# A hybrid decoder block on one core: a fixed order for the output projection, weight loads divided between two queues, rotary steps on VectorE, and compression low parts by adding DMA

## The chip, the cores and the metric

One core of one Trainium2 chip. The metric is the device time of one execution in microseconds, the median of several runs. A second execution is recorded by the hardware profiler, and all rows shown come from it. Engines are named PE (TensorE matmul), PEld (TensorE weight load), DVE (VectorE), ACT (ScalarE), POOL (GpSimd) and SP (SyncE, which here only issues DMAs).

## The reference

512 tokens of width 2048 pass one decoder block. A conditioning vector gives shift, scale and gate vectors (`mod`); one projection feeds two groups of eight heads, forgetting attention (FoX) and native sparse attention (NSA), whose outputs are normalised, concatenated and projected.

```python
def _compress(x, cmp_pos, w1, w2, idx):          # NSA, once for keys, once for values
    blk = x[:, idx] + cmp_pos[None, None, :, None, :]
    blk = blk.transpose(0, 1, 3, 2, 4).reshape(B, idx.shape[0], G, CMP_LEN * D)
    return jax.nn.gelu(blk @ w1) @ w2
...
    mod = jax.nn.silu(c) @ w_ada[l] + b_ada[l]
    sh1, sc1, g1, sh2, sc2, g2 = jnp.split(mod, 6, axis=-1)
    u = _modulate(_rmsnorm(h, norm_attn[l]), sh1, sc1)
    z = u @ w_in                                   # 16 heads' queries, keys, values, gates
    y_f = _rmsnorm(o_f.reshape(B, S, FOX_HEADS * HEAD_DIM), beta_fox)
    y_n = _rmsnorm(o_n.reshape(B, S, NSA_HEADS * HEAD_DIM), beta_nsa)
    h = h + g1[:, None, :] * (concatenate([y_f, y_n]) @ w_out)
    u = _modulate(_rmsnorm(h, norm_ffn[l]), sh2, sc2)
    h = h + g2[:, None, :] * _swiglu(u, w_gate[l], w_up[l], w_down[l])
```

The NSA queries and two of its key sets are rotated (`_rope`). D_MODEL 2048, 8 + 8 heads of 128, compression weights of 32 x 128 rows by 256 columns for keys and again for values, D_FF 5632.

## The kernel before

Activations lie with channels on partitions and 512 tokens along the free axis. Every large product is made of three matmuls on operands split in two: a high part, rounded by an ACT copy (`wh`, `uh`, L244), and a low part, the rest, by a DVE subtraction (`wl`, L249). `gemm` (L289) walks over pieces `ct` of 256 input rows: `load_w` (through `fetch_w`, L218) loads a weight piece on SP's queue into one of three buffers `wr` and splits it, then the matmuls follow. Between pieces `pump` takes a step of a side job: `side_ada` makes the modulation vectors (`ada_block`, L380 loads 512 KB, L386 multiplies and adds on DVE), `side_cmp` the compressions, `att` the attention items, `side_mix` the normalised head outputs. Up to the output projection the scheduler orders each engine's instructions by the program and by when they can be ready; a queue runs its own in order.

The places that the change touches, in time order:

- `z_qn(0)` (L727), queries of the first four NSA heads. `roped` (L606) takes four heads one after another: two ACT copies of the swapped halves, a DVE product (L611), two POOL steps (L612, L613), an ACT high part (L615) and a DVE low part (L616).
- The value products `p_v0` (L744), eight pieces with 288 columns, with `compress` (keys, then values, L655) pumped beside them. A compression has 16 steps: each loads 256 KB (`w1`, L672, on SP), splits it (`evac_pair`, L621 on ACT and L622 on DVE) into a pair from a ring of six (`pair("k", 6, ...)`) and feeds six matmuls (L678). Three of the six pairs hold keys at that time.
- The last value GEMM (`pr == 3`). `mix_hook` pumps `mix_nsa`, which reloads an NSA head's output from DRAM (`reload`, L956, SP), multiplies it by the row scale on POOL (`mix_chunk`, L948) and makes `y`'s high part on ACT (L950) and low part on DVE (L951).
- The output projection. Groups of four or two column blocks of 128 (`out_group`). The first halves of g0 and g1 (rows 8 to 15 of y, the NSA heads) run before the attention pools close; g1's hook `fox_hook` reloads and mixes the FoX heads, every other one on POOL. Then the loop L1193 finishes g0 and g1 and does three whole groups; `x_hook` reloads the hidden state (`hT`, from `xsp`, on SP) and in the last two groups starts the feed-forward's first weights (`w_load`, `w_sums`, `x_high`, `x_low`, `s_split`). After each group `res_add` (L1064, DVE) adds the gated residual, and `hT` is stored to `hsd` by POOL.
- From there a fixed program order (`manual_schedule`) holds for the feed-forward. Its low parts `lx` are made by an ACT pass with factor -1 (L1096) and a POOL DMA that adds the raw weights (L1097).

Of the kernel before, what the change touches and what calls it, by code (L numbers as in the profile page):

```python
# [79 lines left out]
def hymba_block(ctx: ExitStack, tc: tile.TileContext, x, c, positions, w_ada, b_ada, norm_attn,  # L80
# [525 lines left out]
    def roped(src, dst, scale, ct, snt, n):  # L606
# [5 lines left out]
        nc.gpsimd.tensor_tensor(sw, sw, snt, op=OP.mult)  # L612
        nc.gpsimd.tensor_tensor(r, r, sw, op=OP.add)  # L613
# [40 lines left out]
    def compress(which, w1, w2d):  # L654
        hb = bank("s", (P, 256))  # L655
        for s in range(2):
# [26 lines left out]
        nc.sync.dma_start(w2, w2d.rearrange("(m p) n -> p m n", p=P))  # L683
# [43 lines left out]
    def z_qn(g, nxt, **kw):  # L727
        Z = [bank("mm") for _ in range(4)]
        gemm([cols(w_in, C_QN + 512 * g, 512)], u, ND, [("ws", i * P, P, Z[i]) for i in range(4)], **kw)
        w = nxt()  # L730
        if g == 0:
            for i in range(4):
                nc.vector.tensor_tensor(part[:, i, :], part[:, i, :], Z[i], op=OP.add)
        for i in range(4):
            qn[4 * g + i] = pair("q", 6, "qn")
            roped(part[:, i, :] if g == 0 else Z[i], qn[4 * g + i], SCALE, cosT, sinT, T)
        return w
# [5 lines left out]
    w_v0 = z_qn(0, lambda: ahead(p_v0, extra=wsm), k0=ND // 2, start=ND // 2, first=z_first)  # L743
# [5 lines left out]
    gemm(p_v0, u, ND, [("as", 0, 288, bks)], extra=wsm, n_cmp=7, first=w_v0)  # L749
# [40 lines left out]
    side_ada.extend(ada_block(pa, sec, j) for sec, j in todo_ada[:9])  # L790
# [163 lines left out]
    def reload(i):  # L954
        o = sc_tile("or")
        nc.sync.dma_start(o, osp[i])  # L956
        return o
# [12 lines left out]
    def mix_hook(ct):  # L970
        if ct >= 1:
            pump(side_mix, 1 if ct == 1 else 2)
# [38 lines left out]
    pump(side_mix, 1000)  # L1011

    def out_group(i0, n, tags):
        Z = [bank(t) for t in tags[:n]]
        return [cols(w_out, i0 * P, n * P)], y, ND, [("ws", m * P, P, Z[m]) for m in range(n)]

    order = list(range(8, 16)) + list(range(8))
    g0 = out_group(0, 4, BANKS_A)
    gemm(*g0, order=order, n_ada=1, n_att=1.25, k1=8)
    att.drain()  # L1020
    rb = rows_of(sum_rstd(osum[0], FH * HD, "o", "rsf"), "o", q_tmp("rbf"))
    fox = order[8:]

    def fox_hook(ct):
        for h in fox[2 * ct:2 * ct + 2]:
            mix_chunk(reload(h), h, rb)

    g1 = out_group(4, 2, BANKS_B)
    gemm(*g1, order=order, n_ada=1, k1=8, hook=fox_hook)
    pump(side_ada, 1000)  # L1030
# [45 lines left out]
    def w_load(s):  # L1076
        g, k = divmod(s, KG)
        c = slice(g * HT, (g + 1) * HT)
        raw[s] = ring1.tile([P, 4, HT], F32, tag="raw", name=uid("raw"), bufs=6)
        nc.sync.dma_start(raw[s][:, 0:2, :], wu_v[:, :, k, c])  # L1080
        nc.sync.dma_start(raw[s][:, 2:4, :], wg_v[:, :, k, c])
# [110 lines left out]
    side_ada.extend(ada_block(pf, sec, j) for sec, j in todo_ada[9:])  # L1192
    for i0, n, g in ((0, 4, g0), (4, 2, g1), (6, 4, BANKS_A), (10, 4, BANKS_B), (14, 2, BANKS_A)):  # L1193
        k0 = 8 if i0 < 6 else 0
        if i0 >= 6:
            g = out_group(i0, n, g)

        def x_hook(ct):
            if ct == k0 // 2 + 2:
                for i in range(i0, i0 + n):  # L1200
                    nc.sync.dma_start(hT[i], xsp[i])
            if i0 == 10 and 2 <= ct < 8:
                w_load(ct - 2)
            if i0 == 14:
                if ct == 2:
                    hsum["b"] = bank("s")
                    sum_tok(hsum, hsum["t"], True, False)
                if 1 <= ct < 3:
                    w_sums(ct - 1)
                if 1 <= ct < 4:  # L1210
                    x_high(ct - 1)
                if 1 <= ct < 5:
                    x_low(ct - 1)
                if 3 <= ct < 5:
                    s_split(ct - 3)
                if ct == 5:
                    w_sums(2)

        gemm(*g, order=order, k0=k0, hook=x_hook, n_ada=1)
        res_add(i0, [o[3] for o in g[3]], 2, hsum, "hsum")  # L1220
        for i in range(i0, i0 + n):
            nc.gpsimd.dma_start(hsd[i], hT[i])
# [8 lines left out]
    ms = ExitStack()  # L1231
    ms.enter_context(tc.manual_schedule())
# [194 lines left out]
```

## Time and profile before

| | us |
|---|---|
| runs of the kernel before | 2450.6, 2454.54, 2454.8 |
| their median | 2454.54 |
| the profiled execution | 2450.92 |
| its span in the trace | 2448.0 |
| TensorE busy in the span | 2355.1 (96%) |
| DVE, ACT, POOL busy | 1579.6, 1016.0, 341.5 |

The profiled execution's time is 2.9 us longer than its span, the part outside the first and last recorded instruction. A busy time is the sum of an engine's recorded instructions. The granted clock is given as a share of full speed: 1.00 is 2.4 GHz and a stretch at 0.50 would be all at 1.2 GHz. Stretches are named by microseconds from the span's start.

### The profile page before, as it was taken

What the parts mean: (1) busy time and instruction counts of PE and PEld (TensorE: products, weight loads), DVE (VectorE), ACT (ScalarE), POOL (GpSimd) and SP (SyncE); (2) the same over time, 40 slices, a digit from 0 to 9 for tenths busy, and PEclk for the clock granted to TensorE, in tenths of its full rate; (3) what the DMA queues carried; (4) which work ended last, traced back from release to release, by engine and by line L of the source; (5) the groups of instructions that cost most, each with busy time, mean ns of one, the idle gap of its engine ahead of it and who ended that gap; (6) DMA issues with size and microseconds to landing.
All of it is one profiled execution on the core that took longest, in us unless ns stands there. A gap on an engine that the chain in (4) does not pass through costs nothing.

```text
span 2448.0 us, 38482 instructions
## 1 busy us (share of the span) xinstructions
PE 2355.1 (96%) x14717; PEld 2100.4 (86%) x14717; DVE 1579.6 (65%) x2711; ACT 1016.0 (42%) x1531; POOL 341.5 (14%) x370
## 2 busy tenths in 40 slices
PE   6998999999999989889999999999999999999998
PEld 4677887888888767789999999999999888888887
DVE  6876786887755576596777777777776643333333
ACT  3224544344423332365555555555555422222133
POOL 0003002000001121251222121212221100000010
PEclk8998999999999999999999999999999999999999
DMA  9864743463554277559898989898988644333322
GB/s 332 283 198 147 205 139 95 130 190 117 180 174 129 85 249 253 186 122 237 211 231 215 228 213 232 220 225 212 221 200 193 192 151 141 123 120 121 102 95 101
DMA packets 322713, 440.31 MB, mean 180 GB/s; under 512 B 26224, under 2 KB 217552, under 8 KB 322528
## 3 DMA queue, kind: packets, MB, share of 16 engines
q1 hardware_dynamic: 289104, 348.21, 44.0%
q0 software_dynamic: 31120, 85.45, 18.7%
q10 hardware_dynamic: 2304, 4.20, 0.5%
q8 instruction: 115, 1.88, 0.3%
q14 instruction: 70, 0.57, 0.1%
HBM read 340.18 MB, written 28.38 MB: 151 GB/s over the span
## 4 chain that ended last, share of the span: by engine, by line
PE 54%; DVE 1%; DMA 0%; issue 0%; ACT 0%; SPq 0%; DVEq 0%; ACTq 0%
PE py L1161 12%; PE py L1164 11%; PE py L1163 11%; PE psmm L278 3%; PE psmm L279 3%; PE psmm L280 3%; PE pss L278 2%; PE pss L279 2%; PE pss L280 2%; PE pso L279 1%; PE pso L278 1%; PE pso L280 1%; DMA wr<-in_w_down_dram 0%; PE pso L1058 0%; DVE ul L1141 0%
## 5 line engine op out<-in xcount | busy, mean ns | idle before, releaser
L249 DVE TENSOR_TENSOR wl<-wr,wh 128x1024 fp32r<-128x1024 f32 (+2 forms) x211 | 239.0, 1133 | 381.5 <-ACT wh L244 378.4
L244 ACT CAST wh<-wr 128x1024 fp32r<-128x1024 f32 (+2 forms) x211 | 199.5, 948 | 502.7 <-PE psmm L279 199.7
L1164 PE MATMUL py<-uh,ls 128*128 128x256 f32 x1408 | 397.6, 282 | 3.6 <-DVE ls L1107 3.6
L1163 PE MATMUL py<-ul,hs 128*128 128x256 f32 x1408 | 397.6, 282 | 2.2 <-DVE ul L1141 2.2
L1161 PE MATMUL py<-uh,hs 128*128 128x256 f32 x1408 | 398.4, 283 | 1.0 <-DVE ev L1178 0.5
L1107 DVE TENSOR_TENSOR ls<-sum,hs 128x1024 fp32r<-128x1024 f32 x176 | 215.2, 1223 | 196.5 <-ACT hs L1101 196.5
L1101 ACT CAST hs<-sum 128x1024 fp32r<-128x1024 f32 x176 | 184.5, 1049 | 377.3 <-PE py L1163 257.5
L1163 PE MATMUL py<-ul,hx 128*128 128x256 f32 x1056 | 298.8, 283 | 4.0 <-DVE ul L1141 4.0
L1161 PE MATMUL py<-uh,hx 128*128 128x256 f32 x1056 | 299.3, 283 | 1.7 <-ACT uh L1140 1.4
L1164 PE MATMUL py<-uh,lx 128*128 128x256 f32 x1056 | 298.3, 282 | 0.0
L1164 PEld LDWEIGHTS py<-uh,ls 128*128 128x128 f32 x1408 | 267.0, 190 | 4.7 <-DVE ls L1107 4.6
L1163 PEld LDWEIGHTS py<-ul,hs 128*128 128x128 f32 x1408 | 267.0, 190 | 3.3 <-DVE ul L1141 3.3
L1161 PEld LDWEIGHTS py<-uh,hs 128*128 128x128 f32 x1408 | 267.1, 190 | 2.7 <-DVE ev L1178 1.3
L1097 POOL DMA_DIRECT2D lx<-raw x176 | 156.2, 887 | 580.2 <-ACT lx L1096 419.4
L1163 PEld LDWEIGHTS py<-ul,hx 128*128 128x128 f32 x1056 | 200.8, 190 | 5.1 <-DVE ul L1141 5.1
L1161 PEld LDWEIGHTS py<-uh,hx 128*128 128x128 f32 x1056 | 200.6, 190 | 2.2 <-ACT uh L1140 1.7
L1164 PEld LDWEIGHTS py<-uh,lx 128*128 128x128 f32 x1056 | 200.7, 190 | 0.0
L386 DVE SCALAR_TENSOR_TENSOR acc<-ad,sl,acc 128x512 f32<-128x512 f32 x180 | 141.6, 787 | 43.2 <-DMA ad<-in_w_ada_dram 41.4
L1092 ACT CAST hx<-raw 128x768 fp32r<-128x768 f32 x176 | 144.3, 820 | 11.3 <-DMA raw<-in_w_gate_dram 11.3
L1096 ACT ACTIVATE lx<-raw 128x768 fp32r<-128x768 f32 x176 | 148.1, 841 | 1.8 <-DMA raw<-in_w_gate_dram 1.8
L278 PE MATMUL psmm<-fh,wh 128*128 128x512 f32 x352 | 137.0, 389 | 0.0
L280 PE MATMUL psmm<-fh,wl 128*128 128x512 f32 x352 | 136.9, 389 | 0.0
(441 smaller groups left out, 5284.3 us busy)
## 6 DMA issues: line engine op xcount, KB each, us to landing
lx<-raw POOLq DMA_DIRECT2D x176, 384.0 KB, 5.2
ad<-in_w_ada_dram SPq DMA_DIRECT2D x128, 512.0 KB, 4.1
raw<-in_w_up_dram SPq DMA_DIRECT2D x176, 256.0 KB, 4.2
raw<-in_w_gate_dram SPq DMA_DIRECT2D x176, 256.0 KB, 4.5
wr<-in_w_down_dram SPq DMA_DIRECT2D x88, 512.0 KB, 3.6
ad<-in_w_ada_dram SPq DMA_DIRECT2D x128, 256.0 KB, 6.0
wr<-in_w_in_dram SPq DMA_DIRECT2D x104, 256.0 KB, 3.5
wr<-in_w_in_dram SPq DMA_DIRECT2D x24, 512.0 KB, 4.4
```

Source lines behind the costliest of these rows:

```text
L244: nc.scalar.copy(wh[:, :, sc], v)
L249: nc.vector.tensor_tensor(held[1][:, :, sc], v, split_ap(held[0])[:, :, sc], op=OP.subtract)
L278: nc.tensor.matmul(dst, wh[:, k, w], ah, start=first, stop=False)
L279: nc.tensor.matmul(dst, wh[:, k, w], al, start=False, stop=False)
L280: nc.tensor.matmul(dst, wl[:, k, w], ah, start=False, stop=last)
L1096: nc.scalar.activation(lx[s], raw[s][:, 1:4, :], AF.Copy, scale=-1.0)
L1097: nc.gpsimd.dma_start(split_ap(lx[s]), raw[s][:, 1:4, :], accum_op=OP.add)
L1101: nc.scalar.copy(hs[s], sums[s])
L1107: nc.vector.tensor_tensor(ls[s], sums[s], split_ap(hs[s]), op=OP.subtract)
L1161: nc.tensor.matmul(o, wh[:, wi, js], vh[:, vi, :], start=k == 0 and j == 0, stop=False, skip_group_check=True)
L1163: nc.tensor.matmul(o, wh[:, wi, js], vl[:, vi, :], start=False, stop=False, skip_group_check=True)
L1164: nc.tensor.matmul(o, wl[:, wi, js], vh[:, vi, :], start=False, stop=k == KG - 1, skip_group_check=True)
```

## The change

1. Ropes: for the first four NSA heads the two POOL steps go to DVE, and each head's rope is emitted behind one of the first four pieces of the value products. Two of these pieces are loaded ahead, not one.
2. Compression: its weights are loaded by POOL's queue. For every second step the low part is made by a second ACT pass (factor -1) and a POOL DMA that adds the raw weights; the other steps keep the DVE subtraction. Steps are pumped from the fifth piece of the value products on (nine a piece), not from the second and third (seven).
3. One chunk of NSA output per piece in the last value GEMM, not two; the rest in the first w_out group. Reloads go on POOL's queue. Ten modulation blocks before w_out, not nine.
4. From g1 on the fixed program order holds: weight pieces loaded and split one ahead, FoX heads in pairs on DVE alone, the residual of a group after the first products of the next, hidden-state reloads and the first six feed-forward weight pieces on POOL's queue.

```diff
-            pump(side_cmp, n_cmp if ct > 1 else ct)
+            pump(side_cmp, n_cmp if ct > 3 else 0)
...
-    def roped(src, dst, scale, ct, snt, n):
+    def roped(src, dst, scale, ct, snt, n, eng=None):
...
-        nc.gpsimd.tensor_tensor(sw, sw, snt, op=OP.mult)
-        nc.gpsimd.tensor_tensor(r, r, sw, op=OP.add)
+        eng.tensor_tensor(sw, sw, snt, op=OP.mult)
+        eng.tensor_tensor(r, r, sw, op=OP.add)
...
-                nc.sync.dma_start(wr.rearrange("p (l n) -> p l n", n=256),
+                nc.gpsimd.dma_start(wr.rearrange("p (l n) -> p l n", n=256),
...
-                evac_pair(wr, w)
+                if l0 % 4:
+                    nc.scalar.copy(w[0], wr)
+                    nc.scalar.activation(w[1], wr, AF.Copy, scale=-1.0)
+                    nc.gpsimd.dma_start(split_ap(w[1]), wr, accum_op=OP.add)
+                else:
+                    evac_pair(wr, w)
...
-    w_v0 = z_qn(0, lambda: ahead(p_v0, extra=wsm), ...)
+    w_v0, rope_hook = z_qn(0, lambda: ahead(p_v0, extra=wsm) + ahead(p_v0, 1, extra=wsm), ...)
-    gemm(p_v0, u, ND, [("as", 0, 288, bks)], extra=wsm, n_cmp=7, first=w_v0)
+    gemm(p_v0, u, ND, [("as", 0, 288, bks)], extra=wsm, n_cmp=9, first=w_v0, hook=rope_hook)
...
-    side_ada.extend(ada_block(pa, sec, j) for sec, j in todo_ada[:9])
+    side_ada.extend(ada_block(pa, sec, j) for sec, j in todo_ada[:10])
...
     def reload(i):
-        nc.sync.dma_start(o, osp[i])
+        nc.gpsimd.dma_start(o, osp[i])
...
-            pump(side_mix, 1 if ct == 1 else 2)
+            pump(side_mix, 1)
...
+    ms.enter_context(tc.manual_schedule())
+    fox = {h: reload(h) for h in range(4)}
+    g1 = out_group(*groups[1])
+    products(g1, 0, w1[0])
+    r = sum_rstd(osum[0], FH * HD, "o", "rsf")
+    w1.append(load_out(4, 2))
+    products(g1, 1, w1[1])
+    rb = rows_of(r, "o", q_tmp("rbf"))
...
+    w1.append(load_out(4, 3))
+    fox_pair(0)
+    products(g1, 2, w1[2])
+    w0 = [load_out(0, 4)]
+    fox_pair(2)
...
     def w_load(s):
+        eng = nc.gpsimd if s < 6 else nc.sync
...
+        for ct in range(c0, 8):
+            if ct < 7:
+                nw = load_out(i0, ct + 1)
+            elif n_grp < 4:
+                nw = load_out(groups[n_grp + 1][0], starts[n_grp + 1])
+            pump(side_ada, ct in n_ada.get(i0, ()))
+            products(g, ct, w)
+            w = nw
+            if ct == c0 and owed is not None:
+                owed()
+            if ct == (7 if i0 == 0 else c0 + 2):
                 for i in range(i0, i0 + n):
-                    nc.sync.dma_start(hT[i], xsp[i])
+                    nc.gpsimd.dma_start(hT[i], xsp[i])
```

Three places in the order of instructions. First SP's queue at the second half of the first w_out pieces (`wr` are weight pieces, `or` the reloaded FoX heads). Before:

```order
L225 DMA wr_8208<-in_w_out_dram 128x2x256
L956 DMA or_8225<-osp 128x512
L956 DMA or_8232<-osp 128x512
L225 DMA wr_8239<-in_w_out_dram 128x2x256
L956 DMA or_8257<-osp 128x512
L956 DMA or_8264<-osp 128x512
L225 DMA wr_8271<-in_w_out_dram 128x2x256
```

After, on the same queue:

```order
L225 DMA wr_8217<-in_w_out_dram 128x2x256
L225 DMA wr_8222<-in_w_out_dram 128x2x256
L225 DMA wr_8289<-in_w_out_dram 128x2x256
L225 DMA wr_8314<-in_w_out_dram 128x2x256
L225 DMA wr_8345<-in_w_out_dram 128x2x512
L225 DMA wr_8377<-in_w_out_dram 128x2x512
```

The reloads between the weight pieces are gone from SP; they stand on POOL's queue.

Second the compression's loads (`w`) and low parts (`w1l`). Before, on SP, between the value weights (`wr`):

```order
L672 DMA w_360_1914<-in_w_kc_dram 128x2x256
L672 DMA w_363_1926<-in_w_kc_dram 128x2x256
L672 DMA w_366_1938<-in_w_kc_dram 128x2x256
L225 DMA wr_1974<-in_w_in_dram 128x2x128 x2
L672 DMA w_372_1983<-in_w_kc_dram 128x2x256
```

After, on POOL:

```order
L673 DMA w_363_1972<-in_w_kc_dram 128x2x256
L673 DMA w_366_1985<-in_w_kc_dram 128x2x256
L679 DMA w1l_1907<-w_350_1904 128x512
L673 DMA w_369_1997<-in_w_kc_dram 128x2x256
L673 DMA w_372_2010<-in_w_kc_dram 128x2x256
L679 DMA w1l_1975<-w_363_1972 128x512
L673 DMA w_375_2022<-in_w_kc_dram 128x2x256
L673 DMA w_378_2035<-in_w_kc_dram 128x2x256
L679 DMA w1l_2000<-w_369_1997 128x512
```

One adding DMA stands behind every two loads, and the load of a piece stands two adding DMAs before its own.

Third TensorE in the second half of the key compression after the change: one step with an adding DMA (`w1h_1974`, `w1l_1975`), value products (`psmm`) between its high and its low part.

```order
L684 MATMUL pss_1807<-w1h_1974,cA_1950 63x256
L684 MATMUL pss_1807<-w1h_1974,cA_1951 63x256
L283 MATMUL psmm_1639<-wh_2087,uh_1214 128x288
L284 MATMUL psmm_1639<-wh_2087,ul_1215 128x288
L285 MATMUL psmm_1639<-wl_2088,uh_1214 128x288
L283 MATMUL psmm_1636<-wh_2226,uh_1347 128x288
L284 MATMUL psmm_1636<-wh_2226,ul_1348 128x288
L285 MATMUL psmm_1636<-wl_2227,uh_1347 128x288
...
L684 MATMUL pss_1807<-w1l_1975,cA_1950 63x256
```

Before, value products stand between the compression's matmuls in a like way, but 72 rows of value products come ahead of the first compression row, where now 126 do; 66 then stand among the 16 steps of the key compression and 30 rows of the next products behind it, and 13 steps of the value compression follow with none between.

## Rows read from the trace of the kernel before

**Rows 1.** The page's head: span, then busy time, share and instructions per engine.

```profile
span 2448.0 us, 38482 instructions
PE 2355.1 (96%) x14717; PEld 2100.4 (86%) x14717; DVE 1579.6 (65%) x2711; ACT 1016.0 (42%) x1531; POOL 341.5 (14%) x370
```

**Rows 2.** The table by stretch; its first line names the columns.

```profile
core 0: us, PE busy (x) PEld busy (x) DVE busy (x) ACT busy (x) POOL busy (x), PEclk, DMA share, GB/s
217.00:231.00 14.00, 7.28 (x39) 6.32 (x38) 11.69 (x12) 7.45 (x15) 11.60 (x8) 0.76 0.18 56
231.00:255.00 24.00, 23.51 (x171) 22.29 (x170) 19.23 (x34) 15.09 (x29) 0.00 (x0) 0.93 0.75 226
...
265.00:282.00 17.00, 15.56 (x121) 13.85 (x120) 12.37 (x19) 10.98 (x23) 0.00 (x0) 1.00 0.76 228
...
790.00:805.00 15.00, 10.30 (x67) 9.80 (x66) 11.44 (x10) 6.17 (x11) 9.43 (x6) 0.77 0.51 165
...
845.00:870.00 25.00, 20.49 (x93) 15.62 (x92) 15.86 (x23) 11.51 (x18) 6.36 (x4) 0.93 0.50 159
...
890.00:900.00 10.00, 7.68 (x27) 5.88 (x26) 8.15 (x9) 2.92 (x5) 5.40 (x6) 0.83 0.76 252
900.00:945.00 45.00, 44.40 (x198) 36.00 (x198) 27.26 (x32) 10.26 (x11) 3.88 (x4) 1.00 0.77 259
945.00:1000.00 55.00, 51.46 (x220) 40.94 (x219) 36.42 (x46) 18.70 (x22) 11.14 (x12) 0.97 0.90 278
...
1041.00:1100.00 59.00, 51.30 (x396) 48.11 (x395) 57.02 (x86) 39.06 (x62) 32.28 (x33) 1.00 0.50 118
```

**Rows 3.** Groups by form, 217 to 293 us: xcount | busy us, mean ns | idle before.

```profile
L678 PE MATMUL pss<-w1h,cA 128*63 128x256 f32 x128 | 23.7, 281 | 0.8 <-ACT w1h L621 0.7
L622 DVE TENSOR_TENSOR w1l<-w,w1h 128x512 fp32r<-128x512 f32 x32 | 21.6, 690 | 6.2 <-ACT w1h L621 4.7 <-PE pss L678 1.0
...
L621 ACT CAST w1h<-w 128x512 fp32r<-128x512 f32 x32 | 19.5, 620 | 8.8 <-PE pss L678 5.6 <-DMA w<-in_w_kc_dram 2.2 <-DMA w<-in_w_vc_dram 0.3
...
L612 POOL TENSOR_TENSOR sw<-sw,sinT 128x512 f32<-128x512 f32 x4 | 6.6, 1640 | 11.7 <-DVE part L733 11.7
L613 POOL TENSOR_TENSOR r<-r,sw 128x512 f32<-128x512 f32 x4 | 6.1, 1520 | 0.3
...
L616 DVE TENSOR_TENSOR qnl<-r,qnh 128x512 fp32r<-128x512 f32 x4 | 4.9, 1232 | 0.4
```

**Rows 4.** What TensorE waited for, 215 to 293 us: us, times, longest.

```profile
PE psmm L283 <- ACT wh L244: 4.1, 1, 4.1
PE psmm L283 <- DVE part L733: 1.3, 1, 1.3
```

**Rows 5.** DMA issues by group, whole span: count, KB each, median us to landing.

```profile
lx<-raw POOLq DMA_DIRECT2D x176, 384.0 KB, 5.2
ad<-in_w_ada_dram SPq DMA_DIRECT2D x128, 512.0 KB, 4.1
...
w<-in_w_vc_dram SPq DMA_DIRECT2D x16, 256.0 KB, 3.6
...
hsd<-hT POOLq DMA_DIRECT2D x16, 256.0 KB, 2.7
```

**Rows 6.** Line L1097, POOL's adding transfers: duration ns min/median/max, first and last start.

```profile
L1097 POOL DMA_DIRECT2D lx<-raw x176: 847/849/1180, 969.5 to 1918.8; - x176
...
DMA to landing us min/median/max: 3.9/5.2/8.2
```

**Rows 7.** Groups by form, last value GEMM, 786 to 805 us.

```profile
L948 POOL TENSOR_TENSOR or<-or,rbn 128x512 f32<-128x512 f32 x8 | 12.7, 1620 | 19.3 <-ACT rbn L177 19.3
```

**Rows 8.** What TensorE waited for, 785 to 805 us.

```profile
PE psmm L283 <- ACT wh L244: 2.7, 1, 2.7
```

**Rows 9.** What ACT waited for in w_out, 845 to 1027 us.

```profile
ACT wh L244 <- DMA wr<-in_w_out_dram: 59.7, 17, 7.4
```

**Rows 10.** Groups by form, 845 to 1027 us: the modulation products on DVE.

```profile
L386 DVE SCALAR_TENSOR_TENSOR acc<-ad,sl,acc 128x512 f32<-128x512 f32 x45 | 37.3, 829 | 18.3 <-DMA ad<-in_w_ada_dram 17.6
```

More of the change, by code (lines that the diff above doesn't have):

```diff
@@ L733, in z_qn, with rope @@
                 nc.vector.tensor_tensor(part[:, i, :], part[:, i, :], Z[i], op=OP.add)
+        def rope(i):
+            qn[4 * g + i] = pair("q", 6, "qn")
+            roped(part[:, i, :] if g == 0 else Z[i], qn[4 * g + i], SCALE, cosT, sinT, T,
+                  nc.vector if g == 0 else nc.gpsimd)
+        if g == 0:
+            return w, lambda ct: rope(ct) if ct < 4 else None
         for i in range(4):
-            qn[4 * g + i] = pair("q", 6, "qn")
-            roped(part[:, i, :] if g == 0 else Z[i], qn[4 * g + i], SCALE, cosT, sinT, T)
+            rope(i)
         return w
@@ L1010, in hymba_block @@
         att.step()
-    pump(side_mix, 1000)
     def out_group(i0, n, tags):
         Z = [bank(t) for t in tags[:n]]
-        return [cols(w_out, i0 * P, n * P)], y, ND, [("ws", m * P, P, Z[m]) for m in range(n)]
+        return p_out[i0], y, ND, [("ws", m * P, P, Z[m]) for m in range(n)]
     order = list(range(8, 16)) + list(range(8))
-    g0 = out_group(0, 4, BANKS_A)
-    gemm(*g0, order=order, n_ada=1, n_att=1.25, k1=8)
-    att.drain()
-    rb = rows_of(sum_rstd(osum[0], FH * HD, "o", "rsf"), "o", q_tmp("rbf"))
@@ L1022, in hymba_block, with load_out @@
[L1022 to L1029, printed above, removed]
-    pump(side_ada, 1000)
+    groups = [(0, 4, BANKS_A), (4, 2, BANKS_B), (6, 4, BANKS_A), (10, 4, BANKS_B), (14, 2, BANKS_A)]
+    p_out = {i0: [cols(w_out, i0 * P, n * P)] for i0, n, _ in groups}
+    def load_out(i0, ct):
+        return load_w(p_out[i0], order[2 * ct] // 2)
@@ new lines, in products @@
+    def products(g, ct, w):
+        gemm(*g, order=order, k0=2 * ct, k1=2 * ct + 2, first=[lambda: w])
+    g0 = out_group(*groups[0])
+    gemm(*g0, order=order, n_ada=1, n_att=1.25, k1=8, hook=lambda ct: pump(side_mix, 2 if ct == 0 else 1000))
+    w1 = [load_out(4, ct) for ct in range(2)]
+    att.drain()
+    pump(side_ada, 1000)
+    ms = ExitStack()
+    ms.enter_context(tc.manual_schedule())
+    fox = {h: reload(h) for h in range(4)}
+    g1 = out_group(*groups[1])
+    products(g1, 0, w1[0])
@@ L1031, in hymba_block @@
+    w1.append(load_out(4, 3))
[3 more added lines that the diff above has]
+    fox_pair(2)
+    products(g1, 3, w1[3])
+    w0.append(load_out(0, 5))
+    fox_pair(4)
+    products(g0, 4, w0[0])
+    w0.append(load_out(0, 6))
+    fox_pair(6)
+    products(g0, 5, w0[1])
     spare.clear()
@@ L1191, in hymba_block @@
     hsum = {"n": 14}
[L1192 to L1199, printed above, removed]
+    side_ada.extend(ada_block(pf, sec, j) for sec, j in todo_ada[10:])
+    w, owed = w0[2], None
+    starts = [6, 4, 0, 0, 0]
+    n_ada = {4: range(4, 8), 6: range(8), 10: range(4), 14: (2,)}
+    for n_grp, (i0, n, tags_) in enumerate(groups):
+        g = (g0, g1)[n_grp] if n_grp < 2 else out_group(i0, n, tags_)
+        c0 = starts[n_grp]
+        for ct in range(c0, 8):
[9 more added lines that the diff above has]
+            if ct == (7 if i0 == 0 else c0 + 2):
                 for i in range(i0, i0 + n):
-                    nc.sync.dma_start(hT[i], xsp[i])
-            if i0 == 10 and 2 <= ct < 8:
-                w_load(ct - 2)
+                    nc.gpsimd.dma_start(hT[i], xsp[i])
+            if i0 == 10 and ct >= 3:
+                w_load(ct - 3)
             if i0 == 14:
[L1205 to L1213, printed above, removed]
+                if ct == 0:
+                    w_load(5)
+                if ct in (1, 2, 5):
+                    w_sums({1: 0, 2: 1, 5: 2}[ct])
+                if ct in (1, 3, 5):
+                    x_high(ct // 2)
+                if ct in (2, 4, 6, 7):
+                    x_low((2, 4, 6, 7).index(ct))
                 if 3 <= ct < 5:
@@ L1216, in x_hook, with owed @@
                 if ct == 5:
[L1217 to L1222, printed above, removed]
+                    hsum["b"] = bank("s")
+                    sum_tok(hsum, hsum["t"], True, False)
+        def owed(i0=i0, n=n, g=g):
+            res_add(i0, [o[3] for o in g[3]], 2, hsum, "hsum")
+            for i in range(i0, i0 + n):
+                nc.gpsimd.dma_start(hsd[i], hT[i])
+    owed()
     pump(side_ada, 1000)
@@ L1230, in hymba_block @@
     aw.close()
-    ms = ExitStack()
-    ms.enter_context(tc.manual_schedule())
     kk = ExitStack()
```

21 lines of the change are left out of this document (17 added, 4 removed).

## The prediction

> **What bounds the kernel now.** I read the page's totals first. TensorE is busy 96% of the 2448.0 us span, DVE 65% [rows 1], so only the few per cent in which TensorE waits or runs at a low granted clock can be won, unless its work changes, and it does not: the change removes no matmul. Then the table by stretch, over the four places the diff touches [rows 2]. Four things are to be seen there. Around the first value products, 217 to 231 us, TensorE is busy 7.28 us of 14 at a clock of 0.76. The two compressions after them run almost full (23.51 of 24 and 15.56 of 17). The last value GEMM has 10.30 of 15 at 0.77. The w_out GEMMs idle in pieces: 25 - 20.49 = 4.5, 10 - 7.68 = 2.3, 0.6 and 3.5, together 11.0 us, with dips of the clock to 0.93, 0.83 and 0.97. From 1041 on TensorE idles 7.7 us in 59 while DVE is busy 57.02. That tail and the feed-forward after it do the same work before and after; I price them at 0, within 2 either way.
>
> What 0.2% is here: 4.9 us, about what a measurement of this kernel can tell from no change. The sum is made against the profiled execution, 2450.9 us; the median of the three runs shown, 2454.5, lies 3.6 above it. I add half of that, 2, to turn a profiled time into a median.
>
> **Part 1, the four ropes: -7 us (-10 to -3).** Before, POOL does two multiplications per head ahead of the value products, eight in all: 6.6 us plus 6.1 [rows 3], one after another. ACT's next cast stands behind the rounded copy of the rotated head, which waits for POOL; the first matmul waits 4.1 us for that cast and another 1.3 for DVE [rows 4]. The rows show POOL and DVE in each other's way: DVE's low part of a rotated head takes a mean of 1232 ns, the same shape in the compression, with POOL idle, 690 ns [rows 3]. Afterwards the eight steps run on DVE at some 0.69 each, 8 x 0.69 = 5.5 us, one head behind each of the first four pieces of the value products, of which two are loaded ahead. DVE gives back 4 x (1.23 - 0.69) = 2.2 us on the low parts alone, so its load rises by 3.3 us at most; DVE is busy 11.69 of 14 there now, but with waits for POOL in between. TensorE idles 14 - 7.28 = 6.7 us in the stretch, and 0.24 of its busy time plus 0.07 of the next 23.5 us is lost to the clock: 1.7 + 1.6 = 3.4. All of it is 10; the least is the 4.1 wait less 1. I take 7, since the wait for the sum of the head parts (1.3) stays and one cast must still come first.
>
> **Part 2, the compressions: +11 us (+3 to +23).** Each of 32 steps loads 256 KB of weights, makes a rounded high part on ACT (620 ns), a low part on DVE (690 ns) and feeds six matmuls [rows 3]; at 15.56 us for 121 instructions [rows 2] these take 6 x 0.13 = 0.77 us. After the change every second step replaces DVE's 0.69 by a second ACT pass (0.62, taken from the first) and a 256 KB adding transfer from POOL. Its landing time L is the unknown. The nearest rows: POOL's adding transfers of 384 KB land in 5.2 us (3.9 to 8.2), POOL's plain 256 KB in 2.7 [rows 5, 6]. Scaled by bytes the first gives 5.2 x 256/384 = 3.5. I take 4.2, between 3.5 and 5.2, since weights keep 0.75 of the DMA engines busy here [rows 2].
>
> In both kernels three pairs of weight tiles are free for these steps, so a step starts when TensorE has done the third one before it. With DMA steps (D) and DVE steps (E) in turn, a D waits for the E three steps before it, and that E's matmuls follow those of the D four steps before. So from a D to the fourth step after it there run two ACT passes 1.24, L, the four matmuls that follow the low part 0.51 and E's 0.77: a period of L + 2.5 = 6.7 us per four steps. From the order after: three steps are ready before the first; 13 steps of compression 0 stand among 66 value matmuls, 10.0 + 8.6 = 18.6 us of work against 13/4 x 6.7 = 21.8, idle 3.2. Then 30 other matmuls refill the three pairs; 10 of the 13 bare steps of compression 1 give 16.8 against 7.7, idle 9.1. The last three lie among value products. Together 12.3, less the 0.5 + 1.4 that TensorE idles there before [rows 2]: +10.4. For hand-overs between four engines, and a clock that may fall while TensorE is half busy, I round up to +11. By the same sum L = 2.7 gives 0 + 5.3 - 1.9 = +3, and L = 6.3 gives 10.0 + 14.3 - 1.9 = +22, with hand-overs +23.
>
> The Trainium skill has a rule that makes this cheaper ("DMA: Bandwidth & Descriptors", section "Anatomy of one DMA — SWDGE (gpsimd) path"): a POOL-issued DMA costs about 2.0 us plus its bytes at 436 GB/s, as an estimate 2.6 us for 256 KB, by which the term would be about +3. The 2.7 of the plain transfer agrees with it, the 5.2 of the adding one does not, and I let the row decide.
>
> The weight loads themselves move from SP's queue to POOL's. POOL computes nothing there now (0.00 busy from 231 to 255 and from 265 to 282 [rows 2]) and an issue holds it for 849 ns at 384 KB [rows 6]. 32 loads and 16 adding transfers make 48 x some 0.6 to 0.85 = 29 to 41 us over some 55: the queue is hardly a bound. A load can stand behind an adding DMA that waits for ACT; by the order rows of POOL it is issued four steps ahead of its use, a period of 6.7, and such a load lands in 3.6 [rows 5], so this costs nothing by itself. SP's queue, relieved, sends the value weights sooner; what that gives is in part 1.
>
> **Part 3, the last value GEMM: -4 us (-7 to 0).** Eight multiplications on POOL take 12.7 us [rows 7]; ACT's rounded copies wait for them one by one, and a weight cast behind them makes TensorE wait 2.7 [rows 8]. Of 15 us 4.7 are idle, and the clock of 0.77 takes 2.4 more: 7 at most. Afterwards one chunk goes per piece instead of two and the rest falls into the first w_out group, and reloads leave SP for POOL. Against that, the tenth block of modulation weights now runs here, 8 steps of a 512 KB load (4.1 us to landing [rows 5]) and two products of 0.83 us on DVE each [rows 10], 13 us: I take off 3.
>
> **Part 4, w_out: -11 us (-17 to -3).** ACT waits 59.7 us for w_out weights in 17 places [rows 9]; on SP they stand behind reloads which wait for their buffers, as the first order rows show. Now SP carries weights and modulation alone, weights are split one piece ahead, and the loop has 8 modulation steps fewer: 8 x 0.5 MB = 4.2 MB, 15 us of transfer at 278 GB/s [rows 2], and 16 x 0.83 = 13 us of DVE. The four stretches hold 11.0 idle and 0.07 x 20.5 + 0.17 x 7.7 + 0.03 x 51.5 = 4.3 of clock, with the small rests 16 to 17. I take the first and third stretch whole (4.5 + 1.4 + 2.3 + 1.3 = 9.5) and a third of the fourth's 5.0, 1.7: 11. The least is the first stretch but for 1.5. The new costs: all eight FoX multiplications on DVE, 4 more x 0.69 = 2.8 us, in a stretch where DVE is busy 15.86 of 25; the residual add one piece later, which nothing needs before the norm except after the last group, where it is issued at once; hidden-state reloads on POOL behind stores that wait for the previous residual add, needed a group later. In the manual order, an engine that waits holds what stands behind it: DVE's FoX pair waits for a reload, and the next low part stands behind it. That is the bound of -3.
>
> **Sum.** -7 + 11 - 4 - 11 = -11: 2440 for a profiled execution, 2442 as a median.
>
> **Rivals.** (A) *Landing bounds the compression; slower.* Place: the bare steps. Without part 2 the sum is -22, so the point from which it decides is L = 6.3, where part 2 is +23; at 7.2 it is 9.7 per period, 12.9 + 16.6 - 1.9 + 1 = +29, total +7; at the row's maximum of 8.2 +34, total +12. I give 2460 as a median. For: weight loads compete with the adding DMA; against: 256 KB, not 384, and 5.2 as the median. Two free pairs instead of three would do the same. Chance 0.15.
>
> (B) *w_out stays bound by transfer.* From 945 to 1000 the DMA engines are at 0.90 [rows 2]. If the moved loads only share them otherwise, part 4 is -3: total -3, 2448, as a median 2450. Against: fewer bytes. Chance 0.17.
>
> (C) *The adding DMA is nearly as quick as the plain one* (L = 2.7): part 2 is +3, total -19: 2432, as a median 2434. With parts 1 and 4 at their ends 2425, with part 3's too 2422. For: the bytes; against: the 5.2. The rule of the skill quoted above says this case. Chance 0.18.
>
> (D) *DVE holds up POOL's DMAs.* Each adding DMA then waits for one DVE instruction, 0.7 to 1.3 us more: L up to 5.5, part 2 +19, and the reloads likewise some 2: total -1, about 2452 as a median. Against: lx transfers are issued in 847 to 1180 ns while DVE is busy 57.02 of 59 us [rows 2, 6]. The Trainium skill ("SBUF — State Buffer", section "SBUF: two separate sides", the "DVE blocks DMA" trap) states that POOL cannot write descriptors while DVE holds their shared port pair; the issue times speak against its weight here. Chance 0.06.
>
> The forecast keeps 0.44, of which 0.42 is faster. Faster: 0.42 + 0.18 + 0.03 of B = 0.63. Same: 0.02 + 0.14 + 0.06 = 0.22. Slower: 0.15. The range leaves out the far half of C and of A: 2422 to 2460; the forecast's own is 2432 to 2452.
>
> **What would show it.** Right: the first matmul's wait for the cast gone and the clock over 0.9 in the value products; adding transfers landing near 4.2 us and TensorE waiting for them some 12 us in all; TensorE idle under 4 us over w_out. Wrong: landings over 6.3 (A), w_out still idle over 8 us (B), no wait for the adding DMA (C), or, besides, new idle time after 1027, where I put none.

## The result: slower by 0.7%

The changed kernel takes 2470.72 us (median; 2469.08 to 2472.61), the kernel before 2454.67; the ratio is 1.0069, 95% interval 1.0052 to 1.0087. The forecast was 2442, the range 2422 to 2460: wrong, and on the other side.

The page of the changed kernel begins so, in answer to [rows 1]:

```profile
span 2467.3 us, 38518 instructions
PE 2359.9 (96%) x14717; PEld 2104.8 (85%) x14717; DVE 1563.5 (63%) x2707; ACT 1023.1 (41%) x1547; POOL 390.8 (16%) x452
```

The table by stretch, in answer to [rows 2], with the stretches shifted to where the same work now stands: first value products, key compression, its end with the seam and the start of the value compression, the rest of that, last value GEMM, and four stretches of w_out.

```profile
217.00:231.00 14.00, 14.00 (x94) 13.25 (x93) 13.81 (x26) 9.22 (x17) 1.91 (x3) 1.00 0.33 83
...
239.00:262.00 23.00, 18.74 (x144) 17.32 (x143) 8.94 (x16) 14.28 (x29) 13.70 (x17) 1.00 0.87 199
262.00:297.00 35.00, 18.73 (x113) 15.63 (x111) 14.25 (x35) 19.86 (x39) 15.28 (x19) 0.81 0.65 157
297.00:325.00 28.00, 22.55 (x127) 17.85 (x128) 13.70 (x21) 8.27 (x13) 6.81 (x10) 0.87 0.90 253
...
812.00:836.00 24.00, 20.14 (x146) 19.60 (x144) 20.89 (x22) 7.68 (x12) 14.46 (x11) 0.86 0.65 207
...
870.00:895.00 25.00, 24.83 (x127) 20.66 (x126) 13.80 (x24) 11.61 (x17) 3.22 (x6) 1.00 0.47 154
895.00:915.00 20.00, 19.42 (x86) 15.76 (x84) 9.55 (x14) 6.33 (x10) 3.65 (x6) 1.00 0.46 145
915.00:940.00 25.00, 19.66 (x70) 14.61 (x71) 15.80 (x17) 4.94 (x7) 10.40 (x14) 0.86 0.73 242
940.00:1000.00 60.00, 59.28 (x266) 48.97 (x265) 31.00 (x36) 12.95 (x14) 16.51 (x23) 1.00 0.71 237
```

The value products now run without a gap at the full clock, 14.00 of 14 where [rows 2] has 7.28. The stretch with the seam between the two compressions has TensorE at 18.73 of 35 and a granted clock of 0.81. A new hole of 5.3 us stands in w_out at 915 to 940.

Since the order of work differs, equal times are not equal work. So I worked out a **lag**: for each recorded matmul of both profiled executions I summed the columns it streams, and compared the times at which the sums are equal. The heads are times of the kernel before; the number is how much later a kernel is there than the kernel before. Work up to 217 us and from 480 to 780 is the same code in all of them, and differs by up to 4 and 8 us: a difference under some 5 us in one stretch is not to be read from one profiled execution. No head stands between 240 and 480, because there the kernels differ in how many short matmuls they have behind them, and columns mislead: one of 32 columns takes 0.11 us to the next start, one of 256 columns 0.12. Counted by such times and not by columns, the heads given move by less than 1 us.

```
kernel (short label)        217    240    480    780    840    920   1040
changed kernel             +3.7   -6.8  +25.7  +25.7  +26.4  +22.8  +21.0
e1  DVE low parts          +2.2   -8.2   +3.2  +11.1  +11.4   +7.3   +6.2
e2  loads on SP            +2.2   -8.2  +37.3  +43.6  +44.1  +40.5  +36.3
e3  both                   +2.5   -8.0   +3.8   +8.1   +9.3   +4.2   +4.9
e4  front as before        +2.4   +2.3   +4.0   +7.2   +7.7   +2.9   +3.8
e5  ropes two a piece      +3.5   -0.9   +5.6  +12.0  +12.8   +8.8   +6.2
e6  ada later              +3.0   -7.4  +26.6  +29.7  +30.5  +17.7  +16.6
e7  8 adding DMAs          +0.8   -9.6  +17.3  +22.0  +22.6  +18.4  +16.1
e9  e5 and e6 together     +1.7   -2.5   +0.8   +3.4   +3.7   -9.0   -8.4
e10 e4 and e6 together     +1.2   +1.1   +4.2   +7.6   +8.1   -4.6   -5.8
e11 e9, no block at 790    +4.1   -0.4   +7.3   +9.4  +12.0   -0.3   -3.0
e12 10 adding DMAs         +4.1   -6.3  +24.3  +27.1  +30.5  +26.6  +27.2
e13 old ropes, late steps  +3.5   +3.7  +12.3  +14.5  +15.4  +11.2  +10.1
```

By parts, from the first line: ropes -10.5 (217 to 240), compressions and what follows them +32.5 (240 to 480), last value GEMM +0.7 (780 to 840), w_out -5.4 (840 to 1040).

What TensorE waited for from 215 to 350 us in the changed kernel, in answer to [rows 4] (us in total, times, longest):

```profile
PE pss L684 <- DMA w1l<-w: 15.5, 12, 2.9
PE pss L684 <- ACT cA L622: 3.4, 1, 3.4
PE pss L704 <- DVE g L700: 2.5, 1, 2.5
PE pss L788 <- DMA tri<-in_cst_dram: 2.3, 1, 2.3
```

The wait for the cast (4.1 in [rows 4]) is gone. The first line is new: the adding transfers. The other three, 8.2 us together, stand at the seam between the two compressions and behind it: operands of the second (`cA`), the first one's activation (`g`), a constant (`tri`) whose load came late. On SP's queue that load waits for a buffer of the ring that the compression weights pass through, and the next products' weights stand behind it, so that SP issues nothing from 239.4 to 293.1 us:

```profile
SPq L766 <- DMA w<-in_w_vc_dram: 39.4, 1, 39.4
SPq L766 <- DMA w1l<-w: 14.0, 1, 14.0
```

What this costs beyond the 2.3 us no run separates; e1 has such a wait too, of 36.1 us, with 0.7 on TensorE.

The adding transfers themselves, line L679, and two of POOL's waits from 230 to 330 us:

```profile
L679 POOL DMA_DIRECT2D w1l<-w x16: 877/967/992, 234.8 to 317.7; - x16
...
DMA to landing us min/median/max: 3.3/4.5/7.1
```

```profile
POOL w L673 <- DMA w1l<-w: 9.8, 4, 3.6
POOL cumd L797 <- ACT cum L792: 9.3, 1, 9.3
```

They land in 4.5 us, near the 4.2 taken. POOL's own queue waits too: a weight load needs the raw buffer that an adding transfer is still reading, and the last weight loads stand behind stores of cumulative sums (`cumd`) that wait 9.3 us for ACT.

### The profile page after: what moved, and what is told of

Its sections match the earlier page's. It is cut to its first block, busy times and chain, and to the rows that moved or that the text cites. A ratio compares the mean times of both kernels' runs of the same rounds, so it can differ in the third digit from the quotient of the medians.

```text
span 2467.3 us, 38518 instructions
## 1 busy us (share of the span) xinstructions
PE 2359.9 (96%) x14717; PEld 2104.8 (85%) x14717; DVE 1563.5 (63%) x2707; ACT 1023.1 (41%) x1547; POOL 390.8 (16%) x452
## 4 chain that ended last, share of the span: by engine, by line
PE 78%; DVE 8%; DMA 7%; issue 3%; POOL 2%; ACT 2%; SPq 1%; ACTq 0%; DVEq 0%; POOLq 0%
PE py L1210 11%; PE py L1213 11%; PE py L1212 11%; PE psmm L278 7%; PE psmm L280 7%; PE psmm L279 7%; PE pss L278 3%; PE pss L279 3%; PE pss L280 3%; DMA ad<-in_w_ada_dram 2%; DMA wr<-in_w_in_dram 2%; DVE acc L386 2%; PE pso L854 1%; DVE wl L249 1%; DMA wr<-in_w_out_dram 1%
## 5 line engine op out<-in xcount | busy, mean ns | idle before, releaser
L386 DVE SCALAR_TENSOR_TENSOR acc<-ad,sl,acc 128x512 f32<-128x512 f32 x180 | 141.2, 784 | 32.3 <-DMA ad<-in_w_ada_dram 30.6
```

The costliest lines, as they stand in the source:

```text
L386: nc.vector.scalar_tensor_tensor(acc, wr[:, q, :], s, acc, op0=OP.mult, op1=OP.add)
```

## Experiments

The kernel before, timed again beside each set of runs, had medians of 2454.67 to 2458.76, so the text compares ratios. Where a number of an expectation is held against a run below, the ratio is first put on the scale of the result (times 2454.67).

**Who makes the low parts, and who loads** (three runs on the changed kernel). First, DVE makes all low parts (e1):

```diff
-                if l0 % 4:
-                    nc.scalar.copy(w[0], wr)
-                    nc.scalar.activation(w[1], wr, AF.Copy, scale=-1.0)
-                    nc.gpsimd.dma_start(split_ap(w[1]), wr, accum_op=OP.add)
-                else:
-                    evac_pair(wr, w)
+                evac_pair(wr, w)
```

> The changed kernel with every low part of the compression weights made by DVE again; loads stay on POOL's queue, steps are pumped as late as in the change. Landing theory (TensorE waits 15.5 us for adding transfers in the changed kernel, and its clock falls with it): about 20 us come back, 2451 us. Queue theory (weight loads in POOL's in-order queue stand behind adding transfers and behind the cumulative-sum stores): the first half of that goes too, the second stays, about 2458. Placement theory (the steps come too late to be covered, whoever makes the low part): at most 10 come back, 2461 or more.

Measured 2452.27, ratio to before 0.9973 (0.9964 to 0.9983). From 240 to 480 us its lag grows by 11.4 us, the changed kernel's by 32.5: the adding transfers, with the second ACT pass that each needs, cost 21 (by the ratios, 1.0069 less 0.9973, 23.6). TensorE's waits from 215 to 350 us:

```profile
PE pss L679 <- ACT w1h L622: 5.5, 5, 1.5
PE psmm L285 <- DVE wl L249: 1.3, 2, 0.9
PE pss L783 <- DMA tri<-in_cst_dram: 0.7, 1, 0.7
```

Not only is the first line gone; of the 8.2 us at the seam 0.7 are left. The seam itself is as long as ever. From the last matmul of the key compression to the first of the value compression it is 10.9 us before, 11.1 in the changed kernel and 11.9 in e1:

```profile
253.45 0.28 PE L678 MATMUL pss<-w1l,cA 128*63 128x256 f32 x1
264.33 0.28 PE L678 MATMUL pss<-w1h,cA 128*63 128x256 f32 x1
```

```profile
267.74 0.28 PE L684 MATMUL pss<-w1l,cA 128*63 128x256 f32 x1
278.86 0.47 PE L684 MATMUL pss<-w1h,cA 128*63 128x256 f32 x1 [3.43 <-ACT cA L622]
```

```profile
255.42 0.28 PE L679 MATMUL pss<-w1l,cA 128*63 128x256 f32 x1
267.31 0.28 PE L679 MATMUL pss<-w1h,cA 128*63 128x256 f32 x1
```

What differs is the work in between: 68 value products before and 72 in e1, but 24 in the changed kernel, whose slow steps had let the value products run out: the last of them starts at 270.60. So these waits came with the adding transfers too. The landing theory holds for this part. The remaining 11.4 are not the transfers'; a part may be the spread between executions, since e4 and e10, whose front is as before, grow by 1.7 and 3.1 there.

Second, the loads go back to SP (e2), low parts as changed:

```diff
-                nc.gpsimd.dma_start(wr.rearrange("p (l n) -> p l n", n=256),
+                nc.sync.dma_start(wr.rearrange("p (l n) -> p l n", n=256),
...
-        nc.gpsimd.dma_start(w2, w2d.rearrange("(m p) n -> p m n", p=P))
+        nc.sync.dma_start(w2, w2d.rearrange("(m p) n -> p m n", p=P))
```

> The changed kernel with the compression weights loaded by SP's queue again; half the low parts still by adding DMA. Landing theory: 2468 to 2471, the adding transfers still take their 4.5 us. Queue theory: 2458 to 2462. Placement theory: 2468 to 2471.

Measured 2484.72, ratio 1.0111 (1.0096 to 1.0126): worse, which no theory had. SP's waits from 230 to 330 us say why:

```profile
SPq L673 <- DMA w1l<-w: 22.8, 11, 4.3
SPq L673 <- DVE w1l L623: 15.8, 6, 10.2
SPq L673 <- PE pss L710: 7.2, 1, 7.2
```

The load waits for the raw buffer, which an adding transfer holds until it lands, and on SP the value weights and modulation weights stand behind it. Where adding transfers are used, the move of the loads to POOL was a gain.

Third, both undone (e3):

> Both undone: DVE makes all low parts, SP loads; ropes on DVE and the late pumping stay. Landing theory: 2451, like the run with DVE low parts alone. Queue theory: 2446 to 2450, some 8 below that run. Placement theory: 2461 or more, since 13 steps still stand without cover at the end.

Measured 2455.31, ratio 0.9993 (0.9981 to 1.0005), beside 0.9973: without adding transfers POOL's queue is no worse a place than SP's, and the stores in front of the last loads there cost nothing that shows (from 240 to 480 us 11.8, where e1 has 11.4). The queue theory as I had put it falls.

**The front as before** (e4): ropes on POOL, DVE low parts, loads on SP, seven steps a piece from the second piece on; the rest as changed.

> Ropes and compressions wholly as before; the changed reloads, the tenth modulation block and the fixed order of w_out stay. If the stages add up as the two traces show them (the work before 790 us costs +22 of the +16, the last value GEMM +1, w_out -6), this takes 2448 to 2450. If the late stages only gain because the early ones are late (weights ahead), 2455.

Measured 2453.70, ratio 0.9983 (0.9974 to 0.9992). On the result's scale that is 2450.5, the first case. Its lag falls by 3.9 us from 840 to 1040, about the changed kernel's 5.4: the late part gains little by itself.

**Ropes and early steps together** (e5): on e1, two ropes behind each of the first two pieces, steps from the third on, seven a piece.

```diff
-            return w, lambda ct: rope(ct) if ct < 4 else None
+            return w, lambda ct: [rope(i) for i in (2 * ct, 2 * ct + 1) if ct < 2]
...
-            pump(side_cmp, n_cmp if ct > 3 else 0)
+            pump(side_cmp, n_cmp if ct > 1 else 0)
```

> The changed kernel with DVE making all low parts, ropes emitted two behind each of the first two pieces of the value products, and compression steps pumped from the third piece on, seven a piece. Placement theory (without adding transfers the late start of the compressions gives back some 11 us of what the ropes win): most of the 11 return, 2442 to 2445, ratio to before 0.994. Rival (DVE has too much to do once ropes and low parts share it, whatever the order): 2450 to 2453, like the run with the late start.

Measured 2454.19, ratio 0.9980 (0.9967 to 0.9992). From 240 to 480 us it loses 6.5, where e1 loses 11.4, but up to 240 the ropes win only 4.4, where e1 has 10.4: the sum is the same. The placement theory's 0.994 lies outside the interval. The rival's number fits; whether its reason does, DVE having too much to do, is not shown.

**Old ropes, late steps** (e13): on e1, ropes on POOL ahead of the value products, of which one piece is loaded ahead as before.

```diff
-        if g == 0:
-            return w, lambda ct: rope(ct) if ct < 4 else None
...
-                  nc.vector if g == 0 else nc.gpsimd)
+                  nc.gpsimd)
```

> The changed kernel with DVE making all low parts and the ropes as before, on POOL ahead of the value products; the compression steps stay late. If the late start itself costs what the ropes win (some 10 us between the first value products and 400 us): 2461 to 2464, ratio to before 1.002 to 1.004. If the loss after 300 us comes with the ropes' place (their work on DVE pushes DVE's later work back) and not with the late steps: 2452 to 2455, ratio 0.998, like the run with the front as before.

Measured 2462.54, ratio 1.0020 (1.0007 to 1.0032). This is the first case. The ropes' own 10 us are not won; compression loads stay on POOL; and from 240 to 480 us the lag grows by 8.6 all the same, where e4 has 1.7. The first stretch is much as in [rows 2], the loss lies later and is spread:

```profile
217.00:231.00 14.00, 8.76 (x48) 7.55 (x47) 12.98 (x13) 8.23 (x15) 11.09 (x9) 0.88 0.12 27
...
285.00:300.00 15.00, 12.85 (x80) 9.57 (x78) 8.65 (x15) 4.43 (x8) 4.97 (x8) 1.00 0.89 267
```

So four runs make a square, all with DVE low parts: ropes new and steps late 0.9973, ropes old and steps late 1.0020, ropes new and steps early 0.9980, both as before 0.9983. The new ropes are worth 0.5% where the steps are late and nothing that shows where they are early; the late steps cost 0.4% (9 us) beside the old ropes and nothing that shows beside the new. The square is not quite pure, since the last of the four loads on SP. By which engine the late steps cost it is not settled. The first matmuls that use the compressed keys (`kch`), the NSA scores, start at 292.7 us before and at 310.4 in e1:

```profile
L883 PE MATMUL pss<-kch,qnh x32: 262/263/283, 292.7 to 453.8; 128*128 128x32 f32 x32
```

```profile
L891 PE MATMUL pss<-kch,qnh x32: 262/263/263, 310.4 to 456.6; 128*128 128x32 f32 x32
```

It is not the keys that they wait for: those are ready by 267.1 us in e1. In both kernels they start where the value compression ends (its last results are cast from 289.2 to 291.5 us before and from 309.3 to 312.2 in e1).

**How many adding transfers** (two runs on the changed kernel): in every fourth step, eight (e7), and in every third, ten (e12).

```diff
-                if l0 % 4:
+                if l0 % 8 == 2:
```

> The changed kernel with an adding transfer in every fourth compression step, eight in all, not sixteen. Chain theory (a DMA step waits for the DVE step three before it, which follows the DMA step four before; the period per four steps does not depend on the DMA step in between): nearly nothing comes back, 2466 to 2471. Dose theory (each adding transfer costs its own wait of about 1.2 us): half of what the run without them gave back, 2461 to 2463.

```diff
-                if l0 % 4:
+                if l0 % 6 == 2:
```

> The changed kernel with an adding transfer in every third compression step, ten in all. Chain theory (a step starts when the third step before it is done; at every third step that is the adding step itself, so their landings follow one another: 1.24 + 4.5 + 0.5 = 6.2 us per three steps, where every second step gives 7.0 per four): slower than the change by 2 to 8 us, 2473 to 2478. Dose theory: ten sixteenths of the cost, 2463 to 2465.

Measured 2470.48, ratio 1.0048 (1.0030 to 1.0065), and 2470.95, 1.0050 (1.0034 to 1.0065). On the result's scale these are 2466.5 and 2466.9. From 240 to 480 us the lags grow by 26.9 and 30.6; less e1's 11.4 that is 15.5 for eight, 19.2 for ten, 21.1 for sixteen (e12's profiled execution is the slowest of its five, 5.9 us over their median). By the ratios eight cost 0.75%, ten 0.77% and sixteen 0.96% over e1. TensorE's waits for them from 215 to 350 us, e7 and then e12:

```profile
PE pss L684 <- DMA w1l<-w: 11.9, 5, 3.4
```

```profile
PE pss L684 <- DMA w1l<-w: 13.3, 8, 2.9
```

Half the transfers cost three quarters: fewer waits, each longer, 2.4 us against 1.3. The dose theory falls with eight; for ten its 2463 to 2465 is only just too low. The chain theory says the right thing of eight, and was 6 us or more too high for ten. After the fact it can be mended: there the landing's median was 3.7, and 1.24 + 3.7 + 0.51 = 5.5 us per three steps is 1.8 per step, where sixteen with 4.5 give 7.0 / 4 = 1.75, so near equal costs are what it should have said. No run tests that, and whether more free pairs would break the chain was not tried.

**The hole in w_out** (e6). SP's issues, and what ended it on ACT and TensorE, in the changed kernel's timeline (start, duration):

```profile
919.10 0.37 SPq L225 DMA_DIRECT2D wr<-in_w_out_dram  x1
919.70 0.46 SPq L380 DMA_DIRECT2D ad<-in_w_ada_dram  x1
921.80 0.37 SPq L225 DMA_DIRECT2D wr<-in_w_out_dram  x1
```

```profile
920.24 1.54 DVE L386 SCALAR_TENSOR_TENSOR acc<-ad,sl,acc 128x512 f32<-128x512 f32 x2 [0.57 <-DMA ad<-in_w_ada_dram]
```

```profile
925.51 1.04 ACT L244 CAST wh<-wr 128x1024 fp32r<-128x1024 f32 x1 [9.86 <-DMA wr<-in_w_out_dram]
```

```profile
926.61 0.79 PE L278 MATMUL psmm<-yh,wh 128*128 128x512 f32 x1 [4.32 <-ACT wh L244]
```

Weight pieces and modulation weights share one ring of three buffers. The weight load of the next group leaves at 921.80, when DVE is done with the modulation step at 920.24 + 1.54 = 921.78. The short pieces of g1, two column blocks, leave no time for that. The edit:

```diff
-    n_ada = {4: range(4, 8), 6: range(8), 10: range(4), 14: (2,)}
+    n_ada = {6: range(8), 10: range(8), 14: (2,)}
```

> The changed kernel, adding transfers included, with the four modulation steps that fall in the short g1 pieces moved to the second half of the fourth group. Queue theory for the stall at 922 to 927 us (on SP a modulation load waits for its buffer, the weight load of the next group stands behind it): the 8 us lost there come back, 2462 to 2464. Transfer theory (pieces of two blocks need their weights faster than the DMA engines bring them, whatever stands between): 0 to 2 us, 2469 to 2471.

Measured 2468.84, ratio 1.0037 (1.0026 to 1.0048), the changed kernel's being 1.0069. On the result's scale that is 2463.8, the queue theory's number. From 840 to 1040 the lag falls by 13.9, not 5.4. The table by stretch of this kernel:

```profile
910.00:940.00 30.00, 29.39 (x130) 24.02 (x129) 16.05 (x17) 9.66 (x13) 13.15 (x17) 1.00 0.69 239
```

The queue theory holds: over w_out the same bytes are moved, the hole is gone, and the DMA engines are at 0.69 here, with 0.90 reached elsewhere in w_out ([rows 2]).

**The version that beats both** (e9): e5 with that edit.

> The early ropes and compressions without adding transfers, and the modulation steps moved out of g1, together. If both hold as stages: 2435 to 2438, ratio to before 0.991. If only the placement holds: 2443. If neither: 2451.

Measured 2442.43, ratio 0.9934 (0.9920 to 0.9949). The number is nearer the second case, but not for its reason: w_out gives 12.1 us, the front 0.9 from 217 to 480.

**The same without new ropes** (e10): e4 with that edit.

> Ropes and compressions wholly as before, w_out in the fixed order with the modulation steps moved out of g1: the best version so far without its early ropes. If ropes on DVE are worth something once adding transfers are gone: 2446 or more on the scale of that version's 2442, ratio to before 0.995. If their gain is given back by the compressions (the three runs without adding transfers stood 0 to 2 us from before at 480 us): the same 2442, ratio 0.9935.

Measured 2443.88, ratio 0.9950 (0.9934 to 0.9967). The point is the first case's, but the intervals of e9 and e10 overlap, so what the new ropes are worth here (some 0.16%, 4 us) stays open. Most of the gain, if not all, is w_out's.

**The modulation block in the last value GEMM** (e11): e9 without its eight steps there.

```diff
-        gemm(p_vf, u, ND, [("as2", 0, 256, bks)], n_ada=1, n_att=R_V,
+        gemm(p_vf, u, ND, [("as2", 0, 256, bks)], n_ada=0 if pr == 3 else 1, n_att=R_V,
```

> The best version so far without modulation steps in the last value GEMM (four of the eight then fall in the first half of g0, four behind it). If their work on DVE is what ate the gain there: the stretch of that GEMM gains 3 to 5 us and the whole 0 to 3 less what the steps cost in w_out, 2440 to 2443. If not (one reload chain replaces another): no change there, 2443 to 2446.

Measured 2447.58, ratio 0.9962 (0.9948 to 0.9976). From 780 to 800 us the lag falls from +9.4 to +4.5, where e9's goes from +3.4 to +3.2. By 840 it is +12.0: waits in g0's first half, of attention above all, take it back. TensorE's waits from 780 to 830 us, the changed kernel's, e9's and e11's first line:

```profile
PE psmm L285 <- DVE wl L249: 3.5, 1, 3.5
```

```profile
PE psmm L285 <- DVE wl L249: 3.6, 2, 3.4
```

```profile
PE pss L837 <- DVE p L826: 3.6, 2, 2.7
```

What that low part `wl` stands behind on DVE in the changed kernel, with POOL's multiplications beside it (start, duration):

```profile
812.43 8.15 POOL L961 TENSOR_TENSOR or<-or,rbn 128x512 f32<-128x512 f32 x5 [17.30 <-ACT rbn L177]
```

```profile
813.07 3.02 DVE L386 SCALAR_TENSOR_TENSOR acc<-ad,sl,acc 128x512 f32<-128x512 f32 x2 [0.38 <-DMA ad<-in_w_ada_dram]
816.01 3.45 DVE L964 SCALAR_TENSOR_TENSOR yl<-or,vec,yh 128x512 fp32r<-128x512 f32 x2
819.39 1.75 DVE L249 TENSOR_TENSOR wl<-wr,wh 128x512 fp32r<-128x512 f32 x1
821.06 0.74 DVE L386 SCALAR_TENSOR_TENSOR acc<-ad,sl,acc 128x512 f32<-128x512 f32 x1
```

Five of POOL's eight multiplications still run in one block, and while they run a modulation product takes 1.5 us, afterwards 0.74. Without the modulation steps that wait is gone, though a gain of 4.9 us in one profile is at the limit of what can be read. In g0's first half the same steps cost more than that: e11 as a whole is slower than e9 (0.9962 to 0.9934), which neither case had. No third place was tried.

## Why the prediction was wrong, by its own steps

**Part 1 was right in mechanism and short in size.** -7 was taken; the lag falls by 10.5, just past the far end of its range. The cast's wait is gone and the clock is 1.00, as the text asked. But the 10.5 are won only beside late compression steps (4.4 in e5), so this part and the late start of part 2 cannot be priced apart.

**Part 2 is the step that failed: +11 taken, +23 as its upper bound, +32.5 measured.** Its core was sound: L was 4.5 for the 4.2 taken, the waits for adding transfers 15.5 us for the 12.3 worked out. With L = 4.5 the sum itself gives +13. What it left out are three things. It priced only the steps' own operands: "Then 30 other matmuls refill the three pairs" took these 30 as cover enough between the compressions, where the activation and the next operands take 11.1 us one after another. With the late constant that is 8.2 us of waits, of which e1 has 0.7. ("SP's queue, relieved, sends the value weights sooner" held up to 239.4 us only; then SP stood still for 53 us, as shown above.) It rounded a fallen clock up by less than 1; the rows show 0.81 over 18.73 us of work and 0.87 over 22.55, as an estimate 0.19 x 18.73 + 0.13 x 22.55 = 3.6 + 2.9 = 6.5 (in e1, by the same estimate, 2.9 between 240 and 300 us). And it gave the late start no price: "The last three lie among value products" stood there as if that ended it. What comes behind the compressions starts later; e13, whose front differs from before in the late steps and in the loads on POOL, lags 8.6 us more by 480 (e4, with the front as before, 1.7), and its ratio is above e4's by 0.0037, which is 9 us. The three overlap and are not to be added. For the first and the third I had assumed cover without naming it.

**Part 3: -4 taken, +0.7 measured.** The difference is at the limit of what one profile shows. The reloads left SP as said, but POOL's multiplications did not spread out: five run in one block. The price of the tenth block, "I take off 3", was too low. It took 0.83 us for a modulation product from [rows 10], and beside POOL it is 1.5, the effect that part 1 had read from [rows 3]. TensorE's wait for ACT's cast (2.7 in [rows 8]) became one of 3.5 for DVE's low part; without the block e11 gets 4.9 back in the first 20 us.

**Part 4: -11 taken, -5.4 measured.** Within it the first stretches gave what was taken (from 840 to 900 the lag falls from +26.4 to +14.0), and then 8.8 came back up to 920. I had looked at SP's queue for reloads, and not at the modulation loads that stay on it and share the ring; 8.5 of the 13.9 us that e6 gains there hang on where they stand. Over the four stretches of w_out in the table TensorE idles 6.8 us, between the sign for right (under 4) and the one for B (over 8).

**The rivals.** A had the sign, 2460 for 2471, and its place, but not its condition: it decided from a landing of 6.3 us and the landing was 4.5. The slower case was priced through one unknown, when the cover around it was the larger one. C needed a landing of 2.7, D landings towards 5.5; the median of 4.5 speaks against both, though less clearly against D. Against D also stand the issues, 0.88 to 0.99 us each, with no DVE instruction's length added. B named the right part; yet no transfer bound is there: e6 moves the same bytes over w_out without the hole. The Trainium skill's estimate of 2.6 us for such a DMA ("DMA: Bandwidth & Descriptors", section "Anatomy of one DMA — SWDGE (gpsimd) path") is below every one of the sixteen, 3.3 to 7.1, so the trace does not agree here, with other transfers on the engines at 0.65 to 0.90. Nor do the plain weight loads from the same queue there, 3.0 to 6.0, so it is not the adding alone.

## What to carry to other kernels

In a small ring the cost of a slow producer need not go by how often it is used: eight such steps of 32 cost three quarters of what sixteen did, so taking some of them away helped little. Ask too what a slow stream uses up: here it let the value products run out that had covered the seam. When work is moved later, ask what waits for its end and give that a price; a gain in front of it (here 10 us of ropes) and the loss behind it were the same microseconds. Loads that share a buffer ring with the weights are part of the weights' path, on whatever queue they stand: place them where pieces are long.

## What the runs showed of the hardware

An adding transfer of 256 KB within on-chip memory held POOL for 0.88 to 0.99 us and landed in 3.3 to 7.1 us, median 4.5. POOL's plain weight loads of the same size, from the same queue in the same stretch (L673), took 0.72 to 1.12 us to issue and landed in:

```profile
DMA to landing us min/median/max: 3.0/3.9/6.0
```

So the adding one is 0.6 us longer in the median. The 2.7 us of the plain store in [rows 5], from which the prediction read the plain price, is a time from elsewhere in the span. Two of DVE's instructions on 128x512 operands beside POOL's multiplications took 1.5 us (modulation product) and 1.75 us (low part); after them such a product took 0.74, and the low part of that shape is 0.69 with POOL idle ([rows 3]).

The granted clock fell further than I had allowed for where TensorE waited again and again: 0.81 in 262 to 297 us with 18.73 of 35 busy in the changed kernel, and 0.71 in e2 (shares between the two levels, so that a part of each stretch ran at 1.2 GHz):

```profile
239.00:300.00 61.00, 39.56 (x207) 35.58 (x208) 20.45 (x48) 29.48 (x61) 9.91 (x12) 0.71 0.68 160
```

At 0.71, as an estimate (1 - 0.71) x 39.56 = 11.5 us of TensorE's busy time there are owed to the clock, beside the 21.4 us in which it was idle.
